# Attention's probabilities transposed by VectorE squares and transfers through DRAM instead of by TensorE

## The chip, the cores and the metric

The kernel runs on one core of one Trainium2 chip. The metric is device microseconds of one execution; less is better. The engines are named as in the profile: PE is TensorE's matmul (PEld its weight load), DVE is VectorE, ACT is ScalarE, POOL is GpSimd, SP is SyncE. POOL and SP issue the DMAs spoken of here, each from a queue of its own.

## The reference

One decoder block on 512 tokens of width 1024 in float32: an input projection feeds a dilated sliding-window attention and a Mamba-2 mixer, both are gated, summed and projected, and a squared-ReLU MLP follows. The change is in the attention, 12 heads of width 64:

```python
scores = einsum(q, k) * dh ** -0.5 - slope * distance      # causal, three (window, dilation) patterns
p = exp(scores - max)
att = sum over patterns of (p @ v, weighted by its denominator) / sum of the denominators
```

The three patterns see the same keys, so the kernel adds to the scores the distance term and the logarithm of how many patterns hold a pair of positions, and takes one softmax over at most 512 keys.

## The kernel before

Nearly every matrix product is made of float32 operands split into a high and a low half, three matmuls of 128x512 each (`three`, L235; `split`, L95). PE's order is the program's: `mm` and `tr` keep their instructions in program order. DVE, ACT and POOL instructions are placed by the scheduler of the language, by priorities and its own estimate of when things are ready, and each engine then runs its list in order. Weights come by DMA from SP's queue in pieces of 1 MB, double-buffered, and are split by ACT and DVE (`wh_`, `wl_`).

The attention stage lies at about 76 to 232 us of the span. Its work per head `h`:

- `head_scores(h)` (L576): POOL makes a `strip` (distance times slope, L579, plus mask, L580). PE makes the scores of four query tiles of 128 rows, causal, so tile `i` has `(i+1)*128` columns (`pq`, eight matmuls). DVE adds the strip and takes the row extremum (L596), ACT takes the exponential (L598), DVE the reciprocal (L600) and the scaling of four pieces (L603). The result `s` has 1280 columns: query on the partition, key along the row.
- `head_transpose(h)` (L605): PE transposes ten 128x128 squares of `s` into three PSUM banks `pt` (L230 is the helper's line), and ACT copies them to `pT` (L615): key on the partition.
- `pair_values(p)` (L617): for heads `2p` and `2p+1`, PE multiplies `pT` by the values `vtok`, eight matmuls into `po`.

Between these, `fill.run(us)` puts matmuls of input projections (`psq`, `psk`, `psga`, `psgs`, `psz`) into PE's order, up to about that many microseconds by a cost in the code (`FILLA`, `FILLB`, `FILLC`: 3.0, 2.8, 2.8). The loop over heads calls `head_scores(h + 1)`, fills, transposes head `h`, and in every even iteration from 2 on the values of the pair before; the last pair's values lie in `att_unit(0)`, behind its first 15 matmuls (`psap`).

Of the kernel before, what the change touches and what calls it, by code (L numbers as in the profile page):

```python
# [11 lines left out]
F32 = mybir.dt.float32  # L12
F32R = mybir.dt.float32r
AF = mybir.ActivationFunctionType
ALU = mybir.AluOpType
# [3 lines left out]
P = 128  # L19
T = 512  # L20
NT = 4
D = 1024
KD = D // P
NH = 12
# [59 lines left out]
def hybrid_block(ctx: ExitStack, tc: tile.TileContext, a: dict):  # L84
    nc = tc.nc
    act, dve, pool, pe, sp = nc.scalar, nc.vector, nc.gpsimd, nc.tensor, nc.sync
# [139 lines left out]
    def mm(*args, **kw):  # L226
        tc.keep_in_program_order(pe.matmul(*args, **kw))  # L227

    def tr(dst, src):
        tc.keep_in_program_order(pe.transpose(dst, src, ident))  # L230
# [17 lines left out]
    def hbuf(name, dt=F32, tag="hA"):  # L248
        return hp.tile([P, T], dt, name=name, tag=tag)
# [8 lines left out]
    def abank(name):  # L258
        return psa.tile([P, T], F32, name=name, tag="a")
# [8 lines left out]
    vtok = vp.tile([P, NT, AW], F32, name="vtok")  # L268
# [9 lines left out]
    with tc.tile_pool(name="start", bufs=1, reuse_waits="tile") as st:  # L278
# [117 lines left out]
        dist = load_const("dist", [P, T], a["dist"], vp)  # L396
        mask = load_const("mask", [P, T], a["mask"], vp)
# [44 lines left out]
        t = [vp.tile([P, GROUPS, NT, HG], F32, name=f"dt{j}") for j in range(4)]  # L442
# [62 lines left out]

    att = [(hbuf(f"ah{p}", F32R), hbuf(f"al{p}", F32R)) for p in range(NH // 2)]

    SOFF = {3: 0, 2: 512, 0: 896, 1: 1024}
    POFF = {0: 0, 1: 512, 3: 896, 2: 1024}
    BANKS = ((0, 512), (512, 1024), (1024, 1280))  # L510
    actx = ExitStack()
    ap = actx.enter_context(tc.tile_pool(name="attn", bufs=2, side="right", reuse_waits="tile"))

# [57 lines left out]

        return in_unit(f"{n}{d}", evac)

    probs, pT, outs = {}, {}, {}

    def head_scores(h):  # L576

        strip = ap.tile([P, T], F32, name=f"strip{h}", tag="strip", bufs=2)
        pool.tensor_scalar(strip, dist, SLOPES[h], None, ALU.mult)  # L579
        pool.tensor_tensor(strip, strip, mask, op=ALU.add)  # L580
        s = probs[h] = ap.tile([P, 1280], F32, name=f"s{h}", tag="s", bufs=2)
        st = ap.tile([P, 3, NT], F32, name=f"st{h}", tag="st", bufs=2)
        for grp in ((3,), (2, 0), (1,)):
            pq = abank(f"pq{h}_{grp[0]}")
            base = SOFF[grp[0]]
            for i in grp:
                n = (i + 1) * P
                o = SOFF[i] - base
                isl = slice(i * P, (i + 1) * P)
                mm(pq[:, o : o + n], qs[h][:, isl], kh[h][:, 0:n], start=True, stop=False)  # L590
                mm(pq[:, o : o + n], qs[h][:, isl], kl[h][:, 0:n], start=False, stop=True)
            for i in grp:
                n = (i + 1) * P
                o = SOFF[i] - base
                sv = s[:, SOFF[i] : SOFF[i] + n]
                dve.tensor_tensor_reduce(sv, pq[:, o : o + n], strip[:, T - n : T], 1.0, 3e38,  # L596
                                         ALU.add, ALU.min, st[:, 0, i : i + 1])
                act.activation(sv, sv, AF.Exp, bias=st[:, 0, i : i + 1], scale=-1.0,  # L598
                               accum_out=st[:, 1, i : i + 1])
        dve.reciprocal(st[:, 2, :], st[:, 1, :])  # L600
        for i in range(NT):
            sv = s[:, SOFF[i] : SOFF[i] + (i + 1) * P]
            dve.tensor_scalar(sv, sv, st[:, 2, i : i + 1], None, ALU.mult)  # L603

    def head_transpose(h):  # L605
        s = probs.pop(h)
        pT[h] = ap.tile([P, 1280], F32, name=f"pT{h}", tag="pT", bufs=3)
        for b, grp in enumerate(((0,), (1, 3), (2,))):
            b0, b1 = BANKS[b]
            pt = abank(f"pt{h}_{b}")  # L610
            for j in grp:
                for i in range(j, NT):
                    c = POFF[j] - b0 + (i - j) * P
                    tr(pt[:, c : c + P], s[:, SOFF[i] + j * P : SOFF[i] + (j + 1) * P])
            act.activation(pT[h][:, b0:b1], pt[:, : b1 - b0], AF.Copy)  # L615

    def pair_values(p):  # L617
        po = abank(f"po{p}")
        for j in (0, 1, 3, 2):
            n = T - j * P  # L620
            for half in range(2):
                h = 2 * p + half
                mm(po[64 * half : 64 * half + 64, j * P : T], vtok[:, j, h * 64 : (h + 1) * 64],
                   pT[h][:, POFF[j] : POFF[j] + n], start=j == 0, stop=j == 2)
        split(po, att[p][0], att[p][1])
# [353 lines left out]
    for j in range(2):  # L979
        w = take(f"o{j}")  # L980
# [284 lines left out]
    j = last  # L1265
# [49 lines left out]
    for j in range(nu - 2):  # L1315
        w = take(f"dn{j}")
# [55 lines left out]
```

## Time and profile before

| | |
|---|---|
| median of 3 runs | 1086.67 us (1086.59 to 1087.11) |
| the profiled execution, its own time | 1087.34 us |
| its span, first to last instruction | 1085.6 us |
| instructions | 14723 |
| POOL's instructions, busy | 87, 72.0 us |
| DMA moved | 113.06 MB, mean 104 GB/s |

Times in the profile are microseconds from the span's start unless marked ns. Rows of a timeline give start, duration, engine, line and operation, `out<-in`, the shape, and in brackets idle time before it with what ended it; rows of groups give busy time, mean ns of one, and idle time with its releaser. A matmul's duration overlaps the next one's, so steps from start to start tell what it costs. DMA issues do not count as busy time of POOL or SP; the time to landing is counted from the issue.

### The profile page before, as it was taken

To read this page: it belongs to the slowest core of one execution; us is meant where nothing else is said; L and a number is where in the kernel's file an instruction comes from. 1 tells how busy PE (TensorE), PEld (TensorE's weight loads), DVE (VectorE), ACT (ScalarE), POOL (GpSimd) and SP (SyncE) were. 2 spreads that over 40 slices of the span, in tenths; PEclk is the share of its full clock that TensorE was granted. 3 is DMA by queue.
4 is the path that set the end of the run, shared out by engine and by line. 5 is a ranking of instruction groups with operands and counts; after the bars stand their busy time and mean duration, and the time that the engine had idled before them with its cause. 6 is when DMAs were issued, how large, how long until landed. Compare 5 with 4: busy or idle time off the path is not lost.

```text
span 1085.6 us, 14723 instructions
## 1 busy us (share of the span) xinstructions
PE 1074.3 (99%) x5959; PEld 915.7 (84%) x5959; DVE 732.2 (67%) x1096; ACT 535.5 (49%) x921; POOL 72.0 (7%) x87
## 2 busy tenths in 40 slices
PE   9999999999999999999999999999999999999997
PEld 8988787778888888888888878889899998888886
DVE  6657666436777878797979795868677785242324
ACT  6356656526375645547373723454467665332222
POOL 2203122000000010100000000000000000000000
PEclk9999999999999999999999999999999999999999
DMA  8232122322433332333434223540233324333202
GB/s 276 86 100 78 59 78 68 100 76 90 134 88 117 88 126 78 126 83 122 126 103 130 88 80 124 189 160 1 78 117 117 117 80 141 110 120 114 82 35 78
DMA packets 87654, 113.06 MB, mean 104 GB/s; under 512 B 4625, under 2 KB 74769, under 8 KB 86561
## 3 DMA queue, kind: packets, MB, share of 16 engines
q1 hardware_dynamic: 85216, 101.01, 28.9%
q0 software_dynamic: 2224, 11.09, 3.1%
q8 instruction: 47, 0.77, 0.3%
q14 instruction: 23, 0.18, 0.1%
q10 hardware_dynamic: 144, 0.00, 0.0%
HBM read 109.92 MB, written 2.18 MB: 103 GB/s over the span
## 4 chain that ended last, share of the span: by engine, by line
PE 92%; DVE 4%; DMA 2%; ACT 1%; issue 1%; SPq 0%; POOL 0%; POOLq 0%; DVEq 0%; ACTq 0%
PE psd L227 16%; PE psx L227 8%; PE psz L227 8%; PE psbc L227 8%; PE pssp L227 7%; PE psuX L227 6%; PE psu L227 4%; PE psga L227 4%; PE psgs L227 4%; PE psk L227 3%; PE psq L227 3%; PE psuZ L227 3%; PE psv L227 3%; PE psap L227 3%; PE psuY L227 1%; PE pq L227 1%
## 5 line engine op out<-in xcount | busy, mean ns | idle before, releaser
L227 PE MATMUL psd<-wh_dn,hh 128*128 128x512 f32 x240 | 93.4, 389 | 0.0
L227 PE MATMUL psd<-wl_dn,hh 128*128 128x512 f32 x240 | 93.4, 389 | 0.0
L227 PE MATMUL psd<-wh_dn,hl 128*128 128x512 f32 x240 | 93.4, 389 | 0.0
L99 DVE TENSOR_TENSOR hl<-hidden,hh 128x512 fp32r<-128x512 f32 x31 | 21.1, 692 | 71.4 <-ACT hh L96 71.3
L96 ACT ACTIVATE hh<-hidden 128x512 fp32r<-128x512 f32 x31 | 19.1, 628 | 92.0 <-PE psd L227 92.0
L227 PEld LDWEIGHTS psd<-wh_dn,hl 128*128 128x128 f32 x240 | 45.0, 188 | 9.4
L227 PEld LDWEIGHTS psd<-wh_dn,hh 128*128 128x128 f32 x240 | 45.0, 188 | 9.4
L227 PEld LDWEIGHTS psd<-wl_dn,hh 128*128 128x128 f32 x240 | 45.0, 188 | 9.2
L842 ACT ACTIVATE sq<-y 128x512 f32<-128x512 f32 x16 | 17.8, 1120 | 70.5 <-DVE y L839 70.4
L227 PE MATMUL psz<-uh,wh_z 128*128 128x512 f32 x128 | 51.1, 399 | 0.0
L227 PE MATMUL pssp<-yth,wh_sp 128*128 128x512 f32 x128 | 50.9, 398 | 0.0
L227 PE MATMUL psx<-uh,wl_x 128*128 128x512 f32 x128 | 50.0, 390 | 0.7 <-DVE wl_x L99 0.7
L227 PE MATMUL psx<-uh,wh_x 128*128 128x512 f32 x128 | 50.6, 396 | 0.0
L227 PE MATMUL pssp<-yth,wl_sp 128*128 128x512 f32 x128 | 50.1, 392 | 0.0
L227 PE MATMUL psz<-uh,wl_z 128*128 128x512 f32 x128 | 50.0, 391 | 0.0
L227 PE MATMUL pssp<-ytl,wh_sp 128*128 128x512 f32 x128 | 49.9, 390 | 0.0
L227 PE MATMUL psbc<-uh,wh_bc 128*128 128x512 f32 x128 | 49.9, 390 | 0.0
L227 PE MATMUL psz<-ul,wh_z 128*128 128x512 f32 x128 | 49.9, 390 | 0.0
L227 PE MATMUL psx<-ul,wh_x 128*128 128x512 f32 x128 | 49.8, 389 | 0.0
L227 PE MATMUL psbc<-uh,wl_bc 128*128 128x512 f32 x128 | 49.8, 389 | 0.0
L227 PE MATMUL psbc<-ul,wh_bc 128*128 128x512 f32 x128 | 49.8, 389 | 0.0
L693 DVE SCALAR_TENSOR_TENSOR ch<-psx,cw,ch 128x511 f32<-128x511 f32 (+2 forms) x48 | 35.6, 742 | 20.4 <-ACT ch L691 19.7
(361 smaller groups left out, 3253.9 us busy)
## 6 DMA issues: line engine op xcount, KB each, us to landing
ws_up<-in_w_up_dram SPq DMA_DIRECT2D x16, 1024.0 KB, 5.5
ws_dn<-in_w_down_dram SPq DMA_DIRECT2D x15, 1024.0 KB, 5.0
ws_z<-in_w_in_dram SPq DMA_DIRECT2D x8, 1024.0 KB, 7.1
ws_x<-in_w_in_dram SPq DMA_DIRECT2D x8, 1024.0 KB, 5.2
w<-acs_d POOLq DMA_DIRECT2D x8, 1024.0 KB, 5.4
ws_bc<-in_w_in_dram SPq DMA_DIRECT2D x16, 512.0 KB, 4.7
ws_sp<-in_w_ssm_proj_dram SPq DMA_DIRECT2D x8, 1024.0 KB, 4.9
ws_ga<-in_w_in_dram SPq DMA_DIRECT2D x4, 1024.0 KB, 6.2
```

The lines of the kernel that those rows point to most:

```text
L96: ins = act.activation(hi, src, AF.Copy)
L99: ins = (eng or dve).tensor_tensor(lo, src, hi.bitcast(F32), op=ALU.subtract)
L227: tc.keep_in_program_order(pe.matmul(*args, **kw))
L693: dve.scalar_tensor_tensor(h[:, d:], ps[:, : T - d], cw[:, ct, 3 - d : 4 - d], h[:, d:], op0=ALU.mult, op1=ALU.add)
L842: pin(act.activation(q.rearrange("n (j b p) -> n j b p", j=NT, b=4), y.rearrange("n (j p b) -> n j b p", j=NT, b=4), AF.Square, scale=1.0 ...
```

## The change

Line numbers of the changed kernel differ from those of the one before: there L606, L610 and L613 are the DVE steps of the scores, L582 and L583 the strip, L630 the DVE transposes, L635 the writes, L641 the reads.

`head_transpose` now belongs to the end of `head_scores` and holds no PE or ACT work. DVE transposes 32x32 squares of `s` with five instructions into one buffer `sqt` (`bufs=1`, 1536 columns, zeroed once). Eight POOL DMAs write it to two DRAM tiles `p_d`, 32 partitions each; four POOL DMAs read these back into `pT`, so that whole 128x128 blocks end up transposed, with the queries in another order. `pair_values` writes `po` through a strided view, and the split behind it puts the order right. The strip of head `h + 1` is made by `make_strip` at the start of `head_scores(h)`; `s` has one buffer in place of two. The values of a pair come one iteration earlier.

```diff
-    SOFF = {3: 0, 2: 512, 0: 896, 1: 1024}
-    POFF = {0: 0, 1: 512, 3: 896, 2: 1024}
+    SOFF = {1: 0, 0: 256, 2: 384, 3: 768}
+    POFF = {0: 0, 1: 512, 2: 896, 3: 1152}
...
+    sqt = ap.tile([P, 1536], F32, name="sqt", tag="sqt", bufs=1)
+    pool.memset(sqt, 0.0)
...
+    def make_strip(h):
+        strip = strips[h] = ap.tile([P, T], F32, name=f"strip{h}", tag="strip", bufs=2)
         pool.tensor_scalar(strip, dist, SLOPES[h], None, ALU.mult)
         pool.tensor_tensor(strip, strip, mask, op=ALU.add)
...
+    def head_transpose(h, s):
+
+        for n0, tiles, kt in ((SOFF[0], 1, 0), (SOFF[1], 3, 0), (SOFF[1], 3, 1), (SOFF[2], 2, 2), (SOFF[3], 1, 3)):
...
+            dve.transpose(dst, src)
+        rows_ = [dram.tile([2 * P, 4 * w], F32, name=f"p_d{h}_{w}") for w in (P, 64)]
+        for b, w in enumerate((P, 64)):
+            for r in range(4):
+                rs_ = slice(32 * r, 32 * r + 32)
+                pool.dma_start(rows_[b][:, r * w : (r + 1) * w].rearrange("(m i) x -> i m x", i=32),
+                               sqt[rs_, 1024 * b : 1024 * b + 8 * w].rearrange("i (m x) -> i m x", x=w))
         pT[h] = ap.tile([P, 1280], F32, name=f"pT{h}", tag="pT", bufs=3)
-        for b, grp in enumerate(((0,), (1, 3), (2,))):
-            b0, b1 = BANKS[b]
-            pt = abank(f"pt{h}_{b}")
-            for j in grp:
-                for i in range(j, NT):
-                    c = POFF[j] - b0 + (i - j) * P
-                    tr(pt[:, c : c + P], s[:, SOFF[i] + j * P : SOFF[i] + (j + 1) * P])
-            act.activation(pT[h][:, b0:b1], pt[:, : b1 - b0], AF.Copy)
+        for kt in range(4):
+            n = 4 - kt
+            src = rows_[kt // 2][(kt % 2) * P : (kt % 2) * P + P, :].rearrange("p (r x) -> p r x", r=4)
+            pool.dma_start(pT[h][:, POFF[kt] : POFF[kt] + n * P].rearrange("p (r x) -> p r x", r=4),
+                           src[:, :, 32 * (kt % 2) :])
...
-        head_transpose(h)
-        if h % 2 == 0 and h > 0:
+        if h % 2 == 1 and h < NH - 1:
             fill.run(FILLB)
-            pair_values(h // 2 - 1)
+            pair_values(h // 2)
             fill.run(FILLC)
```

The order shows three places. PE, before, where the third head's squares are transposed (`s_1004`, into `pt`) between matmuls of a projection (`psk`):

```order
L227 MATMUL psk_1_1148<-ul,wh_k_960 128x512
L227 MATMUL psk_1_1148<-uh,wl_k_961 128x512
L230 MATMUL pt_0_1159<-ident,s_1004 128x128 x4
L230 MATMUL pt_1_1165<-ident,s_1004 128x128 x4
L230 MATMUL pt_2_1171<-ident,s_1004 128x128 x2
```

PE, now, around the first pair's values (`po`, from `pT` of heads 0 and 1):

```order
L227 MATMUL psk_0_1113<-ul,wh_k_988 128x512
L227 MATMUL psk_0_1113<-uh,wl_k_989 128x512
L227 MATMUL po_1120<-pT_894,vtok 64x512
L227 MATMUL po_1120<-pT_964,vtok 64x512
L227 MATMUL po_1120<-pT_894,vtok 64x4x96
L227 MATMUL po_1120<-pT_964,vtok 64x4x96
L227 MATMUL po_1120<-pT_894,vtok 64x4x32
L227 MATMUL po_1120<-pT_964,vtok 64x4x32
L227 MATMUL po_1120<-pT_894,vtok 64x4x64
```

The groups of `pt` are gone from PE. Between the last score matmul of head 1 and `po` of pair 0 there stand 69 matmuls of projections and the eight of head 2's scores; for the pairs behind it 72, 69, 69 and 66 projection matmuls, and for the last pair 54, with no scores among them. Between the last score matmul of pair `p`'s odd head and the first one of the next odd head there are 81 of them, two groups of scores and one `po`, or a few more.

POOL, before, in the same part of the program: the strips of heads 2 to 4 and nothing else.

```order
L643 DMA acs_d<-acsT 128x128
L579 TENSOR_SCALAR strip_1001<-dist 128x512
L580 TENSOR_TENSOR strip_1001<-strip_1001,mask 128x512
L579 TENSOR_SCALAR strip_1101<-dist 128x512
L580 TENSOR_TENSOR strip_1101<-strip_1101,mask 128x512
L579 TENSOR_SCALAR strip_1234<-dist 128x512
```

POOL, now, around head 3 (`p_d_128_1177`, `p_d_64_1178`, `pT_1187`); `strip_1143` is head 4's, `strip_1268` head 5's:

```order
L641 DMA pT_1073<-p_d_64_1064 128x4x32
L582 TENSOR_SCALAR strip_1143<-dist 128x512
L635 DMA p_d_128_1177<-sqt 32x8x128
L583 TENSOR_TENSOR strip_1143<-strip_1143,mask 128x512
L635 DMA p_d_128_1177<-sqt 32x8x128 x3
L635 DMA p_d_64_1178<-sqt 32x8x64 x4
L641 DMA pT_1187<-p_d_128_1177 128x512
L641 DMA pT_1187<-p_d_128_1177 128x4x96
L641 DMA pT_1187<-p_d_64_1178 128x256
L641 DMA pT_1187<-p_d_64_1178 128x4x32
L582 TENSOR_SCALAR strip_1268<-dist 128x512
```

Twelve DMAs of a head now stand between the strips in POOL's queue, and half of head 4's strip stands behind head 3's first write, which waits for DVE's transposes. The first read waits for the first four writes, the third for the last four.

DVE, before, in head 3 (`s_1104`): the scaling, the low halves of keys (`kl`), then `po`'s low half.

```order
L600 RECIPROCAL st_1105<-st_1105 128x4
L603 TENSOR_SCALAR s_1104<-s_1104,st_1105 128x128
L603 TENSOR_SCALAR s_1104<-s_1104,st_1105 128x256
L603 TENSOR_SCALAR s_1104<-s_1104,st_1105 128x384
L603 TENSOR_SCALAR s_1104<-s_1104,st_1105 128x512
L570 TENSOR_TENSOR kl_1143<-psk_0_1082,kh_1142 64x512 x2
L99 TENSOR_TENSOR al_650<-po_1187,ah_649 128x512
```

DVE, now, in head 3 (`s_1146`):

```order
L613 TENSOR_SCALAR s_1146<-s_1146,st_1147 128x384
L613 TENSOR_SCALAR s_1146<-s_1146,st_1147 128x512
L570 TENSOR_TENSOR kl_1205<-psk_0_1113,kh_1204 64x512 x2
L630 STREAM_TRANSPOSE sqt<-s_1146 128x4x32
L630 STREAM_TRANSPOSE sqt<-s_1146 128x3x4x32 x2
L99 TENSOR_TENSOR wl_q_1250<-ws_q_1247,wh_q_1249 128x1024
L570 TENSOR_TENSOR kl_1236<-psk_1_1210,kh_1235 64x512 x2
L99 TENSOR_TENSOR wl_q_1250<-ws_q_1247,wh_q_1249 128x1024
L630 STREAM_TRANSPOSE sqt<-s_1146 128x2x4x32
L570 TENSOR_TENSOR kl_1242<-psk_1_1210,kh_1241 64x512 x2
L630 STREAM_TRANSPOSE sqt<-s_1146 128x4x32
```

Five transposes came in, with splits of a weight and of keys between them. The first waits until the head before has landed its first four writes, the fourth for the other four, since `sqt` is one buffer; the splits behind a waiting transpose wait with it. In head 7 a weight's and two keys' splits stand between the scaling and the transposes; in heads 5, 9 and 11 there is little or nothing.

More of the change, by code (lines that the diff above doesn't have):

```diff
@@ L506, in hybrid_block @@
     att = [(hbuf(f"ah{p}", F32R), hbuf(f"al{p}", F32R)) for p in range(NH // 2)]
-    SOFF = {3: 0, 2: 512, 0: 896, 1: 1024}
-    POFF = {0: 0, 1: 512, 3: 896, 2: 1024}
-    BANKS = ((0, 512), (512, 1024), (1024, 1280))
+    SOFF = {1: 0, 0: 256, 2: 384, 3: 768}
+    POFF = {0: 0, 1: 512, 2: 896, 3: 1152}
     actx = ExitStack()
@@ L572, in qk_unit, with head_scores @@
         return in_unit(f"{n}{d}", evac)
-    probs, pT, outs = {}, {}, {}
-    def head_scores(h):
-        strip = ap.tile([P, T], F32, name=f"strip{h}", tag="strip", bufs=2)
+    pT = {}
+    sqt = ap.tile([P, 1536], F32, name="sqt", tag="sqt", bufs=1)
+    pool.memset(sqt, 0.0)
+    strips = {}
+    def make_strip(h):
+        strip = strips[h] = ap.tile([P, T], F32, name=f"strip{h}", tag="strip", bufs=2)
         pool.tensor_scalar(strip, dist, SLOPES[h], None, ALU.mult)
         pool.tensor_tensor(strip, strip, mask, op=ALU.add)
-        s = probs[h] = ap.tile([P, 1280], F32, name=f"s{h}", tag="s", bufs=2)
+    make_strip(0)
+    def head_scores(h):
+        strip = strips.pop(h)
+        if h + 1 < NH:
+            make_strip(h + 1)
+        s = ap.tile([P, 1280], F32, name=f"s{h}", tag="s", bufs=1)
         st = ap.tile([P, 3, NT], F32, name=f"st{h}", tag="st", bufs=2)
@@ L584, in head_scores @@
             pq = abank(f"pq{h}_{grp[0]}")
-            base = SOFF[grp[0]]
             for i in grp:
                 n = (i + 1) * P
-                o = SOFF[i] - base
+                o = 3 * P if i == 0 else 0
                 isl = slice(i * P, (i + 1) * P)
@@ L593, in head_scores @@
                 n = (i + 1) * P
-                o = SOFF[i] - base
+                o = 3 * P if i == 0 else 0
                 sv = s[:, SOFF[i] : SOFF[i] + n]
@@ L603, in head_scores @@
             dve.tensor_scalar(sv, sv, st[:, 2, i : i + 1], None, ALU.mult)
-    def head_transpose(h):
-        s = probs.pop(h)
-        pT[h] = ap.tile([P, 1280], F32, name=f"pT{h}", tag="pT", bufs=3)
-        for b, grp in enumerate(((0,), (1, 3), (2,))):
-            b0, b1 = BANKS[b]
-            pt = abank(f"pt{h}_{b}")
-            for j in grp:
-                for i in range(j, NT):
-                    c = POFF[j] - b0 + (i - j) * P
-                    tr(pt[:, c : c + P], s[:, SOFF[i] + j * P : SOFF[i] + (j + 1) * P])
-            act.activation(pT[h][:, b0:b1], pt[:, : b1 - b0], AF.Copy)
+        head_transpose(h, s)
@@ new lines, in head_transpose @@
+    def head_transpose(h, s):
+        for n0, tiles, kt in ((SOFF[0], 1, 0), (SOFF[1], 3, 0), (SOFF[1], 3, 1), (SOFF[2], 2, 2), (SOFF[3], 1, 3)):
+            first = 0 if n0 == SOFF[0] else 4 - tiles
+            src = s[:, n0 + kt * P : n0 + kt * P + (tiles - 1) * 3 * P + P]
+            if tiles > 1:
+                src = bass.AP(tensor=src.tensor, offset=src.offset,
+                              ap=[src.ap[0], [3 * P, tiles], [32, 4], [1, 32]])
+            else:
+                src = src.rearrange("p (q c j) -> p q c j", q=1, j=32)
+            w = P if kt < 2 else 64
+            dst = sqt[:, 1024 * (kt // 2) + 4 * w * (kt % 2) : 1024 * (kt // 2) + 4 * w * (kt % 2) + 4 * w]
+            q0 = first if kt < 2 else first - 2
+            dst = dst.rearrange("p (c q j) -> p q c j", c=4, j=32)[:, q0 : q0 + tiles]
+            dve.transpose(dst, src)
[5 more added lines that the diff above has]
+                               sqt[rs_, 1024 * b : 1024 * b + 8 * w].rearrange("i (m x) -> i m x", x=w))
+        pT[h] = ap.tile([P, 1280], F32, name=f"pT{h}", tag="pT", bufs=3)
+        for kt in range(4):
[3 more added lines that the diff above has]
+                           src[:, :, 32 * (kt % 2) :])
@@ L617, in pair_values @@
     def pair_values(p):
         po = abank(f"po{p}")
+        pov = po.rearrange("p (r x) -> p r x", r=4)
         for j in (0, 1, 3, 2):
@@ L622, in pair_values @@
                 h = 2 * p + half
-                mm(po[64 * half : 64 * half + 64, j * P : T], vtok[:, j, h * 64 : (h + 1) * 64],
-                   pT[h][:, POFF[j] : POFF[j] + n], start=j == 0, stop=j == 2)
-        split(po, att[p][0], att[p][1])
+                mm(pov[64 * half : 64 * half + 64, :, 32 * j :], vtok[:, j, h * 64 : (h + 1) * 64],
+                   pT[h][:, POFF[j] : POFF[j] + n].rearrange("p (r x) -> p r x", r=4), start=j == 0, stop=j == 2)
+        split(po.rearrange("p (r q j) -> p q r j", r=4, q=4), *(t.rearrange("p (q r j) -> p q r j", r=4, q=4)
+                                                                for t in att[p]))
     sz0 = []
```

## The prediction

> **What bounds the kernel now.** I read the busy times and slices first, then the waits, then the timeline of the stage that changes. The page's lines:
>
> ```profile
> span 1085.6 us, 14723 instructions
> PE 1074.3 (99%) x5959; PEld 915.7 (84%) x5959; DVE 732.2 (67%) x1096; ACT 535.5 (49%) x921; POOL 72.0 (7%) x87
> PEclk9999999999999999999999999999999999999999
> ```
>
> TensorE is busy for 99% of the span at full granted clock. The attention stage, from the windows view (PE, PEld, DVE, ACT, POOL busy, clock, DMA share, GB/s), and the longest waits of PE in the whole run:
>
> ```profile
> 12.00:14.00 2.00, 1.25 (x10) 0.84 (x8) 2.00 (x5) 0.92 (x3) 0.00 (x0) 1.00 1.03 404
> 80.00:232.00 152.00, 152.00 (x785) 121.20 (x784) 90.66 (x207) 87.18 (x192) 28.75 (x21) 1.00 0.26 80
> PE warm L227 <- POOL ones L218: 1.2, 1, 1.2
> PE ut L230 <- DVE un L334: 1.1, 1, 1.1
> ```
>
> In those 152 us PE never waits: each PE instruction taken out there shortens the run, and each microsecond that PE is made to wait lengthens it. DVE has 61 us free, POOL over 120 us, DMA three quarters. The first row shows DMA moving 404 GB/s, five times the stage's 80.
>
> **What is removed.** Ten transposes of each head on PE (start, duration):
>
> ```profile
> 121.31 0.39 PE L227 MATMUL psga<-ul,wh_ga 128*128 128x512 f32 x1
> ...
> 124.28 0.39 PE L227 MATMUL psga<-uh,wl_ga 128*128 128x512 f32 x1
> 124.51 1.25 PE L230 MATMUL pt<-ident,s 128*128 128x128 f32 x10
> 125.52 0.48 PE L227 MATMUL psga<-uh,wh_ga 128*128 128x512 f32 x1
> 125.83 0.40 PE L227 MATMUL psga<-ul,wh_ga 128*128 128x512 f32 x1
> ```
>
> The rows from 121.31 to 124.28 are 13 steps of 0.2285 us, the price of a full matmul. From 124.51 to 125.83 are 1.32 us with one full matmul in it, so a group costs 1.09 us, and 12 heads give **-13.1 us**, all on the path. The 36 copies of ACT go too:
>
> ```profile
> L615 ACT ACTIVATE pT<-pt 128x512 f32<-128x512 f32 (+1 forms) x36 | 16.4, 524 | 5.9 <-PE pt L230 5.8
> ```
>
> Their 16.4 us lay beside PE, which did not wait: worth nothing. The values matmuls keep their column counts (512, 384, 256, 128, now in four strided pieces): 0.
>
> **What is added on DVE.** Five transposes a head. The nearest rows: one DVE transpose of 128 columns, and a DVE operation by width:
>
> ```profile
> L854 DVE STREAM_TRANSPOSE pnt<-pn x8: 304/306/317, 304.3 to 655.3; 128x128 f32<-128x128 f32 x8
> L596 DVE CUSTOM_DVE_ANT_0 s<-pq,strip 128x512 f32<-128x512 f32 x11 | 7.6, 688 | 8.3 <-PE pq L227 8.3
> L596 DVE CUSTOM_DVE_ANT_0 s<-pq,strip 128x128 f32<-128x128 f32 x11 | 3.1, 285 | 0.0
> ```
>
> 688 less 285 over three widths is 134 ns per 128 columns, so 306, 574, 574, 440 and 306 ns: 1.45 us for the first three, 2.2 us for all, 26 us in the stage. DVE goes from 91 to 117 of 152 us; PE covers it. Without that cover it is part of the chain below.
>
> **What is added on POOL, and the wait it makes.** Twelve DMAs a head: eight writes of 256 contiguous runs each (512 B or 256 B), then reads of 128, 512, 128 and 512 runs. The trace has only DMAs of 128 runs; POOL's rows, and the time to landing:
>
> ```profile
> 68.58 0.76 POOL L643 DMA_DIRECT2D acs_d<-acsT  x1 [23.38 <-DVE acsT L642]
> 125.24 1.49 POOL L579 TENSOR_SCALAR strip<-dist 128x512 f32<-128x512 f32 x1 [14.34 <-DVE st L596]
> 126.81 1.35 POOL L580 TENSOR_TENSOR strip<-strip,mask 128x512 f32<-128x512 f32 x1
> 306.76 0.61 POOL L859 DMA_DIRECT2D rt_d<-rt  x1 [0.30 <-POOL rt L215]
> 309.41 0.56 POOL L861 DMA_DIRECT2D rg<-rt_d  x1 [2.04 <-DMA rt_d<-rt]
> rg<-rt_d POOLq DMA_DIRECT2D x8, 256.0 KB, 3.6
> rt_d<-rt POOLq DMA_DIRECT2D x8, 2.0 KB, 1.9
> acs_d<-acsT POOLq DMA_DIRECT2D x1, 64.0 KB, 2.8
> ```
>
> A read that depends on a write starts 2.65 us after it (306.76 to 309.41). An issue of 128 runs costs 0.55 to 0.76 us. What 256 and 512 cost is unknown: 0.55 if runs are free; 1.5 and 2.2 if the cost grows with them in full (2 x 0.76, 4 x 0.55). I take 0.76 for a write (acs_d has the same 512 B runs), 0.55 for the plain reads and 0.9 for the cut ones, and keep both ends. How long the scores take to become scaled probabilities, PE's last score matmul and DVE's scaling, in a head with other DVE work between and in one without:
>
> ```profile
> 120.95 0.28 PE L227 MATMUL pq<-kl,qs 128*128 128x256 f32 x1
> 126.46 2.32 DVE L603 TENSOR_SCALAR s<-s,st 128x128 f32<-128x128 f32 x4
> 172.52 0.28 PE L227 MATMUL pq<-kl,qs 128*128 128x256 f32 x1
> 175.48 2.30 DVE L603 TENSOR_SCALAR s<-s,st 128x128 f32<-128x128 f32 x4
> ```
>
> That is 7.5 us (121.23 to 128.78) and 5.0 us. The chain of an odd head, clean: 5.0 scaled, 1.45 three transposes, 1.33 the strip's addition behind the first write on POOL, 8 x 0.76 = 6.1 writes: 13.9 us. The third read waits for the last write, 2.65 after that issue began (13.1): 15.75. Its issue 0.55, the fourth lands 3.6 after its start: **19.9 us**, or 22.4 with other DVE work.
>
> PE's own work from the end of the odd head's scores to `po`: by the order 72, 69, 69 and 66 full matmuls and one group of scores (1.35 us) for pairs 1 to 4, so 17.8, 17.1, 17.1 and 16.4 us. The order puts other DVE work into heads 3 and 7, little into 5 and 9. Waits: 22.4 - 17.8 = 4.6, 19.9 - 17.1 = 2.8, 5.3, 3.5: 16.2 us. Pair 0: heads 0 and 1 score only 5.4 us apart, and POOL serves head 0 first: its writes begin at 84.7 (scores end at 78.1), end at 90.8, third read 92.7, last issue ends 94.1; head 1's writes end at 100.2, its third read starts at 102.1, data at 106.2. PE is there at 83.5 + 17.1 = 100.6: 5.6 us. Last pair: 54 full matmuls, 12.3 us, against 19.9 - 1.33 (no strip left) = 18.6: 6.3 us. Sum of waits **+28.1 us**.
>
> POOL's own sum per head is 6.1 + 1.1 + 1.8 + 2.8 = 11.8 us plus about 1.3 us of waiting for landings, within PE's period of 11.8 us (half of 81 full matmuls, two score groups and 2.4 us of `po`) plus the waits. The single `sqt` makes DVE's next transposes wait until the writes have landed, some 10 us after they were ready; heads are 11 us apart or more, so this holds at these prices, and DVE's queue behind it (the low halves of the weights) is not delayed. Bytes: 1.4 MB a head, 117 GB/s beside 80: under the 404 seen.
>
> **Sum.** -13.1 + 28.1 = +15.0 us. The profiled execution took 1087.34 us (span 1085.6 and 1.7 around it), 0.67 above the median of the runs, so 1102.3 for its like and 1086.67 + 15.0 = **1102 us** as a median.
>
> The Trainium skill, *DMA: Bandwidth & Descriptors*, section on one DMA by the gpsimd path, gives about 2.0 us plus bytes over 436 GB/s per DMA. By it a write lands in 2.3 us and the last read in 2.15, each chain is 1.8 us shorter, and the sum would be about +4 us. The trace's 2.65 and 3.6 us are longer, and its numbers are kept above.
>
> **Rivals.**
> - *Hidden after all (faster).* Issues at 0.55, landings at 1.9 and 2.8, scaling in 4.5: 4.5 + 1.45 + 1.33 + 4.4 = 11.7; third read 13.05; data at 16.4, not later than PE anywhere but at the last pair (15.1 against 12.3: 2.8 us). Net -10 us, 1076. For it: the rows at 0.55 and 1.9. Against: they move less or in longer runs. It decides when the six waits together stay under 13.1 us.
> - *POOL becomes the bound.* Writes at 1.1, cut reads at 1.5: 8.8 + 1.1 + 3.0 = 12.9 us a head and 2.8 for nine strips: 180 us from 84.7, data of head 11 at 267. Without waits `po` of the last pair would start at 214.5 (227.6 before, less 13.1). Net 267 - 227.6 = +39, 1126; with the full doubling some +95. It decides when a head costs POOL more than 13 us, that is a write above 0.85. For it: twice to four times the runs of any row.
> - *PE restarts slowly.* The first matmuls of the kernel, and the same ones later:
>
> ```profile
> 1.16 5.73 PE L227 MATMUL warm<-ones 128*128 128x128 f32 x28 [1.16 <-POOL ones L218]
> 8.64 0.83 PE L227 MATMUL warm<-ones 128*128 128x128 f32 x6
> ```
>
> 28 in 5.57 us (to the next start at 6.73) is 199 ns each, against 0.58 / 6 = 97 ns (8.64 to 9.22): about half pace after standing still. If each of the six waits brings back some 3.5 us at half pace, 1.7 us is lost each time: +10, 1112. For it: waits of 3 to 6 us where before none passed 1.2. The Trainium skill, *TensorE: Matmul & The Clock Gate*, Part 1, states this: half clock after an idle window of about 3.4 us, full after as long a busy one. The 199 ns agree with the cold half.
>
> **Chances.** Forecast, +3 to +30: 0.52. PE restarts slowly: 0.08. POOL-bound: 0.17. Hidden: 0.15. Gain and waits cancel: 0.08. A difference of 0.2% (2.2 us) is about what can be told from no change. So faster 0.15, same 0.08, slower 0.77. The range leaves out a tenth at either end, most of the hidden case below and of the doubled prices above: 1080 to 1148.
>
> **What would show it.** No `pt` on PE; PE idle before six `po`, by DMA `pT`, 3 to 6 us each; POOL's writes near 0.76, cut reads near 0.9; DVE transposes of 0.3 to 0.6 us; the rest of the span as before. Writes at 1 us or more, or DVE waiting for `p_d` ahead of its transposes, would prove me too low; `po` without a wait, too high.

## The result, and the profile after

The changed kernel takes 1104.1 us (median of four, 1101.8 to 1106.6) where the kernel before took 1086.8 beside it: a ratio of 1.0159 with a 95% interval of 1.0137 to 1.0181, 17.3 us slower. The profiled execution took 1103.85 us, its span 1102.0. The lines of the page that answer to those of before (span, busy times, granted clock by slices):

```profile
span 1102.0 us, 14769 instructions
PE 1073.3 (97%) x5839; PEld 907.2 (82%) x5839; DVE 748.0 (68%) x1156; ACT 519.4 (47%) x885; POOL 161.0 (15%) x232
PEclk9999999989999999999999999999999999999999
```

PE has 120 instructions fewer and is busy almost as long as before (1073.3 against 1074.3 us): what it saved is given back as slower work, and the span has 16.4 us more on top. POOL's busy time, other than the section on the profile before says, does count its DMA issues: in the attention stage 56.2 us are writes, 31.5 reads and 28.1 strips. The windows view puts it in the attention stage (PE, PEld, DVE, ACT, POOL busy, clock, DMA share, GB/s), and the view of waits, for that stage, says for what:

```profile
80.00:250.00 170.00, 152.33 (x670) 113.70 (x669) 105.76 (x266) 71.17 (x156) 115.68 (x165) 0.96 0.63 172
PE po L227 <- DMA pT<-p_d: 17.7, 10, 3.2
POOL p_d L635 <- DVE sqt L630: 27.4, 10, 6.2
POOL pT L641 <- DMA p_d<-sqt: 7.0, 8, 2.0
```

Where PE was busy for every microsecond, it is now idle for 17.7 of 170 (170.00 less 152.33), all of it at `po`, for `pT`. The DMA engines' share went from 0.26 at 80 GB/s to 0.63 at 172. POOL, the engine that issues, was busy for 115.68 of the 170 us; most of the rest it stood waiting for DVE, 27.4 us of it for the transposes. From the start of each values group to its end, less the 2.4 us that it takes without a wait, PE lost 5.7, 3.3, 4.1, 6.1, 1.4 and 6.6 us at the six pairs, 27.2 in all; 28.1 had been forecast (5.6, 4.6, 2.8, 5.3, 3.5, 6.3). For 17.7 of these 27.2 us PE stood still; in the other 9.5 it is recorded as busy longer than such groups are elsewhere.

The last pair's chain from end to end, in the order of time (PE's last score matmul, DVE's scaling and transposes, POOL's writes and reads, PE's values):

```profile
223.46 0.28 PE L227 MATMUL pq<-kl,qs 128*128 128x256 f32 x1
226.68 1.27 DVE L613 TENSOR_SCALAR s<-s,st 128x128 f32<-128x128 f32 x4
227.87 0.76 DVE L630 STREAM_TRANSPOSE sqt<-s 128x128 f32<-128x128 f32 x2
228.56 0.65 DVE L543 SCALAR_TENSOR_TENSOR sz<-sz,psz 128x512 f32<-128x512 f32 x1
229.13 1.08 DVE L630 STREAM_TRANSPOSE sqt<-s 128x384 f32<-128x384 f32 x3
229.98 4.63 POOL L635 DMA_DIRECT2D p_d<-sqt  x8 [3.00 <-DVE sqt L630]
235.28 2.70 POOL L641 DMA_DIRECT2D pT<-p_d  x4 [0.67 <-issue]
235.95 1.07 PE L227 MATMUL po<-pT,vtok 128*64 128x512 f32 x2
238.51 1.07 PE L227 MATMUL po<-pT,vtok 128*64 128x512 f32 x4 [1.50 <-DMA pT<-p_d]
241.07 1.14 PE L227 MATMUL po<-pT,vtok 128*64 128x384 f32 x4 [1.48 <-DMA pT<-p_d]
243.42 1.54 PE L227 MATMUL po<-pT,vtok 128*64 128x128 f32 x6 [1.22 <-DMA pT<-p_d]
```

PE's last scores end at 223.74 and the last data lands at 243.38: 19.6 us, where the forecast's chain for this pair was 18.6. Prices of the parts: minimum, median and maximum in ns of one transpose, one write and one read, and median landing times.

```profile
L630 DVE STREAM_TRANSPOSE sqt<-s x60: 262/404/578, 84.7 to 229.9; 128x128 f32<-128x128 f32 x24, 128x384 f32<-128x384 f32 x24, 128x256 f32<-128x256 f32 x12
L635 POOL DMA_DIRECT2D p_d<-sqt x96: 582/584/732, 86.2 to 234.0; - x96
L641 POOL DMA_DIRECT2D pT<-p_d x48: 549/682/767, 91.7 to 237.2; - x48
p_d<-sqt POOLq DMA_DIRECT2D x48, 128.0 KB, 2.8
pT<-p_d POOLq DMA_DIRECT2D x12, 192.0 KB, 3.8
pT<-p_d POOLq DMA_DIRECT2D x12, 64.0 KB, 5.1
```

Issuing was cheaper than taken (a write 0.58, not 0.76; a cut read 0.75, not 0.9), and the last landing dearer: 5.1 us at the median for the fourth read of a head, though it is the smallest. That median hides two cases. The same read behind the same three others lands in 2.3 to 3.0 us in heads 1, 2, 3, 6 and 9, and in 5.5 to 6.1 us in heads 0, 4, 5, 7, 10 and 11. In the six late ones 0.8 to 1.05 MB of weights for the projections, issued by SP, moved while the reads were under way, in the five early ones 0.2 MB or none; head 8 (4.7 us) fits neither. Here are the last two reads in an early head, 3 (DMA view from 131.9 to 135 us), and in a late one, 7, with the weights beside them (185.7 to 192.2):

```profile
pT<-p_d POOLq DMA_DIRECT2D x1, 128.0 KB, 2.2
pT<-p_d POOLq DMA_DIRECT2D x1, 64.0 KB, 2.3
```

```profile
ws_ap<-in_w_att_proj_dram SPq DMA_DIRECT2D x1, 768.0 KB, 6.9
pT<-p_d POOLq DMA_DIRECT2D x1, 128.0 KB, 5.0
pT<-p_d POOLq DMA_DIRECT2D x1, 64.0 KB, 5.8
```

So the last part of a chain meets the weights or misses them. This goes by what the rows show together; no run moved a weight's transfer away. In the last head's stretch the windows view has a DMA share of 0.95 at 270 GB/s:

```profile
235.00:245.00 10.00, 5.81 (x22) 1.93 (x20) 0.78 (x1) 0.00 (x1) 3.14 (x5) 0.83 0.95 270
```

The granted clock fell to 0.50 three times in the stage. The 3.4 us ahead of the first and of the last fall, and the three stretches at the low clock:

```profile
101.60:105.00 3.40, 0.73 (x4) 0.20 (x4) 3.34 (x8) 1.22 (x4) 3.02 (x5) 1.00 0.58 182
238.10:241.50 3.40, 1.50 (x8) 0.40 (x8) 0.00 (x0) 0.00 (x0) 0.42 (x1) 1.00 1.16 300
105.00:108.40 3.40, 3.40 (x13) 1.64 (x12) 2.27 (x11) 1.66 (x7) 0.68 (x1) 0.50 0.95 289
193.70:197.10 3.40, 3.40 (x9) 2.67 (x9) 0.69 (x1) 0.00 (x0) 1.18 (x2) 0.50 0.05 13
241.50:248.30 6.80, 5.58 (x17) 3.46 (x15) 0.69 (x1) 0.60 (x1) 0.00 (x0) 0.50 0.60 203
```

What the second of them costs, after pair 3:

```profile
193.53 0.46 PE L227 MATMUL psga<-uh,wl_ga 128*128 128x512 f32 x1
193.79 0.63 PE L227 MATMUL psga<-uh,wh_ga 128*128 128x512 f32 x1
...
197.18 0.39 PE L227 MATMUL psga<-uh,wl_ga 128*128 128x512 f32 x1
```

From 193.79 to 197.18 eight full matmuls take 0.424 us each instead of 0.2285: 1.6 us lost after the wait has ended. About as much is lost behind the last pair, whose group ends at 244.96; the stretch from 105.0 lies almost whole inside pair 0's group (100.04 to 108.13) and is counted there.

### The profile page after: what moved, and what is told of

Read it like the earlier page. It is cut to its first block, busy times and chain, and to the rows that moved or that the text cites. A ratio compares the mean times of both kernels' runs of the same rounds, so it can differ in the third digit from the quotient of the medians.

```text
span 1102.0 us, 14769 instructions
## 1 busy us (share of the span) xinstructions
PE 1073.3 (97%) x5839; PEld 907.2 (82%) x5839; DVE 748.0 (68%) x1156; ACT 519.4 (47%) x885; POOL 161.0 (15%) x232
## 4 chain that ended last, share of the span: by engine, by line
PE 81%; DMA 6%; DVE 6%; POOL 2%; issue 2%; ACT 2%; POOLq 0%; SPq 0%; DVEq 0%; ACTq 0%
PE psd L227 15%; PE psx L227 8%; PE psbc L227 8%; PE psz L227 8%; PE pssp L227 7%; PE psuX L227 6%; PE psu L227 4%; PE psgs L227 3%; PE psuZ L227 3%; PE psv L227 3%; PE psap L227 3%; DMA pT<-p_d 2%; PE psk L227 2%; DMA p_d<-sqt 2%; PE psga L227 2%
## 5 line engine op out<-in xcount | busy, mean ns | idle before, releaser
L635 POOL DMA_DIRECT2D p_d<-sqt x96 | 56.2, 593 | 27.6 <-DVE sqt L630 27.4
```

The lines of the kernel that those rows point to most:

```text
L635: pool.dma_start(rows_[b][:, r * w : (r + 1) * w].rearrange("(m i) x -> i m x", i=32), sqt[rs_, 1024 * b : 1024 * b + 8 * w].rearrange("i ...
```

## The experiments

Twelve kernels were run, each beside the kernel before on the same chip (1086.9 to 1087.2 us there), so the ratios are compared.

**1 (none). What the removal alone is worth.** The values multiply a constant `pTc`, and nothing is transposed:

```diff
-        head_transpose(h, s)
-                   pT[h][:, POFF[j] : POFF[j] + n]...
+                   pTc[:, POFF[j] : POFF[j] + n]...
```

> The changed kernel without its second half: the probabilities are not transposed at all (no DVE transposes, no writes, no reads), and the values matmuls multiply a constant tile of zeros of the same shape, so nothing waits. The output is therefore not attention's. It prices the removal alone. Theory: 12 groups of ten PE transposes at 1.09 us are gone and nothing comes in their place, so 1086.7 - 13.1 = 1073.6 us (1072.5 to 1075). Rival: PE was held by something else in part of those groups (a weight load, an eviction), so that less comes back: over 1077 us.

Measured: 1073.24 us, ratio 0.9874 (0.9861 to 0.9888), within the theory's range. The page's span, with PE busy for 99% of it again:

```profile
span 1071.5 us, 14445 instructions
PE 1060.4 (99%) x5839; PEld 903.2 (84%) x5839; DVE 732.2 (68%) x1096; ACT 519.8 (49%) x885; POOL 74.6 (7%) x89
```

13.7 us are gained against 13.1 forecast. So the ten PE transposes of a head were all on the path, and what the change puts in their place costs 1104.1 - 1073.2 = 30.9 us.

**2 (nowait). The new work, with nobody waiting for it.** The same constant in the values, but all transposes, writes and reads stay; `pT` has two buffers:

> The changed kernel with all its DVE transposes, writes and reads, but the values matmuls multiply a constant tile of zeros instead of what is read back, so PE never waits for the chain (pT has two buffers instead of three, to make room for the constant; the output is not attention's). Theory: the work on DVE, POOL and the DMA engines hides beside PE, so the time is that of the kernel without it, 1073.6 us (1072.5 to 1076), and all that the changed kernel loses is the wait for the data and what follows from it: 27 us of waiting and some 4 of slow clock. Rival: the side load itself costs PE time, by low halves of the weights that DVE delivers late, by weight or score evictions behind the transposes, or by DMA contention with the weights: 1077 to 1090 us, with waits of PE at places other than po.

Measured: 1095.42 us, ratio 1.0081 (1.0067 to 1.0095). The rival was right in kind, and by more than its range (1077 to 1090): 22.2 us over the run without transposes although PE waits for no read at all. The view of waits of PE in the stage, and the clock by slices:

```profile
PE pq L227 <- DVE st L608: 13.8, 7, 4.1
PEclk9999898999999999999999999999999999999999
```

PE now waits at the scores' banks, which DVE empties late, seven times up to 4.1 us, and in the stage (80 to 232 us) its granted clock is 0.93 on the mean, so part of the loss is slow clock. So the forecast's picture, a chain that is late for PE while DVE and POOL have time to spare, lacks something: the side work alone holds PE up. In the changed kernel the waits view has no such wait; PE, held at `po`, probably came to the scores late enough.

**3 (warm). Does the wait cost clock?** Matmuls of no use fill the waits:

```diff
+        for _ in range({0: 18, 1: 12, 2: 15, 3: 22, 4: 4, 5: 24}[p]):
+            mm(po, uh[:, 0, 0:P], uh[:, 0, :], start=True, stop=True)
```

> The changed kernel with matmuls of no use (18, 12, 15, 22, 4 and 24 of 0.2285 us, into the bank that the values overwrite) in front of the six values groups, where PE waits; each fills most of a wait, so PE is not idle for 3 us anywhere in the stage. Theory that the waits also cost clock: the 0.59 of full clock that the windows show for about 4 us after three of the waits goes, about 1.6 us at each, so 1104.1 - 5 = 1099 us (1097.5 to 1101). Rival, that only the idle time counts and the lower clock in the records has no cost of its own: 1104 us (1102.5 to 1106), or a little more where a dummy group outlasts its wait.

Measured: 1108.5 us, ratio 1.0195 (1.018 to 1.021). Neither: 4.4 us slower. The waits for `pT` fell only from 17.7 to 8.2 us for 21.7 us of added matmuls, because the data came later too: in the first pair the reads of the second head began at 102.5 instead of 101.2 us, and the fourth of them landed at 110.2 instead of 106.4, in 5.8 us instead of 3.0, with 1.05 MB of weights moving beside it instead of 0.2. Every later head starts from there. As a test of the clock it decides nothing; run 12 asks again where nothing follows that depends on PE.

**4 (late). More time for each chain.** The values one iteration of the head loop later, a fourth `pT` buffer, the strips in buffers that only the last pair's output needs:

```diff
-        if h % 2 == 1 and h < NH - 1:
+        if h % 2 == 0 and h > 0:
             fill.run(FILLB)
-            pair_values(h // 2)
+            pair_values(h // 2 - 1)
```

> The changed kernel with the values of a pair one iteration of the head loop later, where the kernel before had them (after the scores of head 2p+3 instead of 2p+2), so that a head's chain has a further PE period of about 11.8 us to end in. That needs a fourth pT buffer; room for it is made by keeping the two strips in two of the heap's buffers that the last pair's output takes only at its end. The last pair is not moved. Theory (the chain's lag, about 19 to 22 us a head, is the cause, and its throughput is enough): the waits of the first five pairs, 20.6 us in the profile, go with their slow clock of about 3 us, the last one of 6.6 us stays: 1104.1 - 23.6 = 1080.5 us (1078.5 to 1083). Rival (POOL's throughput is the cause: some 11.5 us a head with its waits for landings against a PE period that is now 11.8): the waits come back one pair later and at the last pair, which waits for over 12 us: 1086 us or more.

Measured: 1106.73 us, ratio 1.0186 (1.017 to 1.0202): no faster than the change itself. The lag alone, on which my whole sum rested, is refuted as the single cause. The waits of PE, and of DVE for the strips:

```profile
PE po L227 <- DMA pT<-p_d: 14.1, 4, 9.7
PE pq L227 <- DVE st L607: 5.9, 4, 2.1
DVE s L607 <- POOL strip L584: 9.8, 6, 4.6
```

The first five pairs did what the theory said: beyond 2.4 us each, their groups lost 4.8 us together instead of 20.6. The waits came back elsewhere, as the rival said: 12.0 us at the last pair (9.7 and 2.3), 5.9 at the scores, and there DVE had been waiting 9.8 us for strips that stood in POOL's queue behind reads. The rival's reason, that POOL is full, does not follow: in the same stage POOL itself waited 20.2 us for transposes and 14.7 us for writes to land. Head 11's strip, for which DVE waited 4.6 us, began at 220.80; POOL had stood still for 3.6 us just before, at a read whose writes had not landed. It is the order of the queue that these rows show.

**5 and 6 (strip, late_s). POOL's queue relieved.** One edit on the changed kernel (5, with one strip buffer in place of two), and on the kernel of run 4 (6):

```diff
-        pool.tensor_scalar(strip, dist, SLOPES[h], None, ALU.mult)
-        pool.tensor_tensor(strip, strip, mask, op=ALU.add)
+        dve.scalar_tensor_tensor(strip, dist, SLOPES[h], mask, op0=ALU.mult, op1=ALU.add)
```

> The changed kernel with one edit: each head's strip is made by DVE in one instruction (about 0.7 us, one buffer) instead of two by POOL (1.49 + 1.3 us). Theory (POOL's queue is what the heads stand in line for, at some 11.5 us a head): 2.8 us less of POOL per head, and no strip between the first write and the second, shortens every chain by 1.3 us at least, and the six waits at po together by 8 to 14 us: 1104.1 - 11 = 1093 us (1090 to 1097). Rival (POOL is not the limit; DVE, which delivers its transposes late, is, and gets 0.7 us a head more to do): 1102 us or more.

> The kernel of run late (values one head later) with the strips made by DVE instead of POOL. In run late PE waited 5.9 us at the scores' bank, because DVE waited 9.8 us for strips that stood behind reads in POOL's queue, and 9.7 us at the last pair, because POOL was behind by then. Theory (POOL's throughput): without the strips a head costs POOL about 8.7 us with its waits against PE's 11.8, so POOL keeps up: the waits at the scores go, pairs 0 to 4 don't wait, the last waits 5 to 7 us: 1073.2 + 7 and 1 to 3 of slow clock = 1082 us (1079 to 1086). Rival (DVE's late transposes set the chain, whoever makes the strips): 1095 us or more.

Measured: 1097.48 us (ratio 1.0096, 1.0082 to 1.011) and 1089.47 us (1.0021, 1.0012 to 1.003). On the changed kernel the edit is worth 6.6 us, less than the 8 to 14 expected; with the later values it is worth 17, but 1089.47 is above the theory's range (1079 to 1086) and below the rival's 1095. Later values alone gave nothing, the strips alone 6.6, both 14.6: two limits in a row, and lifting the first shows the second. Whether it is the strips' place in the queue or their 2.8 us a head that counts, these two runs do not separate. With both, one long wait is left, at the last pair, and the values after it are slow (14 matmuls in 4.53 us):

```profile
PE po L227 <- DMA pT<-p_d: 11.0, 3, 10.1
227.78 4.53 PE L227 MATMUL po<-pT,vtok 128*64 128x512 f32 x14 [10.11 <-DMA pT<-p_d]
```

**7 (late3). Run 6 with 30 matmuls ahead of the last pair's values instead of 15.**

> As run late_s, and the last pair's values behind 30 matmuls of the first part of the next projection instead of 15, so 3.4 us later on PE. Theory: the last wait shrinks by those 3.4 us and what slow clock follows from it: 3 to 5 us less than late_s, 1078 us (1075 to 1082), faster than the kernel before. Rival: the last wait is not set by the lag but by what DVE and POOL still have in line; then the time is that of late_s within 1 us.

Measured: 1087.42 us, ratio 1.0003 (0.9994 to 1.0012). The last wait fell by 3.9 us to 6.2 in the profile, the median time by 2.1, less than the 3 to 5 expected and more than the rival's 1; the runs of the two kernels overlap (1085.7 to 1089.3 here, 1088.1 to 1090.6 before). Neither forecast was met.

**8 and 9 (nowait_s, nowait_2). What is left of the side load.** Run 2 with the strips on DVE (8), then with two buffers for `s` besides (9; the change had made it one) and, to make room, one for `pT`:

> The kernel of run nowait (all the transposes and transfers are made, but the values multiply a constant tile of zeros, so nobody waits for what is read back; the output is not attention's) with the strips made by DVE instead of POOL. In run nowait PE lost 22 us to the side load, 14 of it in waits at the scores' bank behind DVE. Theory (DVE waits for POOL's queue: for strips, and for sqt to be written out): without the strips the queue is short enough, and the time comes to within 1 to 6 us of the run with no transposes: 1074 to 1080 us. Rival (DVE is blocked by its own order, the transposes and the output's low half standing ahead of the scores): 1088 us or more.

> The kernel of run nowait_s (nobody waits for what is read back; strips by DVE; the output is not attention's), with two buffers for the scores s, as the kernel before the change had, instead of one; pT has one buffer for that. In nowait_s 12.6 us were left over the run without transposes, 8.5 of it waits of PE at the scores' bank for DVE. Theory (with one s DVE can't read the next head's scores out of their banks until all five transposes of this head are through, and these stand behind split work in DVE's queue): with two, the waits at the scores go and the time is within 4 us of the run without transposes, 1074 to 1077 us. Rival (DVE is simply late, or the one sqt blocks it until its writes have landed): 1082 us or more.

Measured: 1085.80 us (ratio 0.9986, 0.9978 to 0.9995) and 1088.99 us (1.0024, 1.0014 to 1.0033). The first lies between theory and rival, the second is in the rival's range. The strips were 9.6 of the 22.2 us; 12.6 remain, 8.5 of them waits at the scores. With two `s` these waits fell to 2.7 us, as the theory said, but the time rose: nobody waits for the transposes in this kernel, so its last ones run at the start of the next stage, whose first work on DVE (`ch`) and whose transfer on POOL (`w`) stand behind them in the order, and PE waits there instead. The rows of DVE and POOL, and the waits of PE from 76 to 290 us in run 9:

```profile
246.04 1.55 DVE L631 STREAM_TRANSPOSE sqt<-s 128x384 f32<-128x384 f32 x4
247.51 3.98 DVE L723 SCALAR_TENSOR_TENSOR ch<-psx,cw,ch 128x511 f32<-128x511 f32 x6
255.60 0.55 POOL L784 DMA_DIRECT2D w<-acs_d  x1
PE ptx L230 <- DVE ct L727: 3.0, 1, 3.0
PE pq L227 <- DVE st L607: 2.7, 2, 1.4
PE psap L227 <- DVE ch L723: 2.4, 1, 2.4
```

So the single `s` is part of how DVE's lateness reaches the scores, and DVE's queue is a second line in which the heads stand; what the single `s` costs the changed kernel by itself stays open, because a kernel with later values has no room for a second `s`.

**10 and 11 (late4, late5). The last wait covered.** Run 7 with 45 matmuls ahead of the last pair's values (10), and less filling work after each head besides, `FILLA` 2.7 for 3.0, so that some of it is left for the end (11):

> As run late3 (values one head later, strips by DVE), with the last pair's values behind 45 matmuls of the next projection instead of 30: five of its six parts of three columns of the output are begun first, in three banks, then the values, then the sixth parts and the fourth column. In late3 PE waited 6.2 us for the last pair, its values group took 4.3 instead of 2.4 us, and the next part waited 0.9 us for the output's halves. Theory: all that is left of the loss is that one wait for the last head's chain, so 15 matmuls of 0.2285 us take 3.4 us from it, and some slow clock: 1083 us (1081.5 to 1084.5), faster than the kernel before by 0.3%. Rival: the last head's chain moves with PE (DVE or POOL are still behind by then), and the time stays at 1086 us or more.

> As run late4, with less of the other projections' work put after each head's scores (FILLA 2.7 instead of 3.0), so that more of it is left for the stretch between the last head's scores and its values: 102 matmuls (23.3 us) by the order, against 69 in late3, where the wait was 6.2 us. Theory: the last wait is covered whole and no other comes, since POOL and DVE need less than a period for a head once the strips are off POOL: 1073.2 and 2 to 4 for the first matmuls at low clock and small waits, 1077 us (1075 to 1080). Rival: with a shorter period (11 us) the heads' throughput on DVE and POOL is the bound again, and waits at the scores and at the earlier pairs give the time back: 1083 us or more.

Measured: 1084.55 us (ratio 0.9979, 0.997 to 0.9987) and 1088.23 us (1.0012, 1.0002 to 1.0021). Run 10, just above its theory's range, beats the kernel before by 0.2%, its last wait down to 3.8 us. Run 11 fell to its rival: the last wait is 1.3 us, but 2.4 came at the second pair, 1.9 at the scores and 1.0 at the fourth pair. With a shorter period the waits come back, so DVE, POOL and the transfers together seem to need about the period that they have; which of them, this run does not tell.

**12 (late4w). Clock, asked where nothing depends on PE afterwards.** Run 10 with 16 matmuls of no use where PE stood still:

```diff
+        for _ in range(16 if p == NH // 2 - 1 else 0):
+            mm(po, uh[:, 0, 0:P], uh[:, 0, :], start=True, stop=True)
```

> As run late4, with 16 matmuls of no use (3.66 us at 0.2285) into the last pair's bank in front of its values, where PE stood still for 3.83 us in late4; nothing before that place depends on PE any more, so the wait itself ends when it did. In late4 the values after the wait took 4.53 us for 14 matmuls at a granted clock of 0.50, against 2.37 us for all 16 elsewhere. Theory (standing still for 3 to 4 us costs clock afterwards, beside the wait): with PE busy through the wait the clock stays up, the values take 2.4 us and what follows runs at full pace: 2.4 us less, 1082.1 us (1081 to 1083.3). Rival (the slow values come from something else than the pause, their data's landing or the strided reading of pT): the time of late4, 1084.5 us (1083.5 to 1085.5).

Measured: 1081.53 us, ratio 0.9949 (0.9936 to 0.9963), about 3 us less than run 10, as the theory said (1081 to 1083.3), and the fastest of the kernels that do all the work. The values after the wait in run 10, its window from 229.2 to 233, and the same places of run 12:

```profile
229.26 4.53 PE L227 MATMUL po<-pT,vtok 128*64 128x512 f32 x14 [3.83 <-DMA pT<-p_d]
229.20:233.00 3.80, 3.74 (x13) 2.14 (x14) 0.00 (x0) 0.00 (x0) 0.14 (x1) 0.50 0.92 314
```

```profile
223.30 3.79 PE L227 MATMUL po<-uh 128*128 128x512 f32 x16
227.02 3.02 PE L227 MATMUL po<-pT,vtok 128*64 128x512 f32 x16
229.20:233.00 3.80, 2.89 (x15) 1.84 (x15) 1.44 (x3) 0.85 (x2) 0.00 (x0) 1.00 0.56 226
```

With PE kept busy the clock is 1.00 where it was 0.50, and the values take 3.02 us for 16 (0.65 more than elsewhere) instead of 4.53 for 14. In run 10 the last data landed at 230.86 us and the group ended 2.9 us later; in run 12 it landed at 229.13 and the group ended 0.9 us later. So standing still for 3.8 us costs about 2 us more afterwards by these rows. The times of the two runs differ by 3, but in the two profiled executions the last data also came 1.7 us earlier, so not all of the 3 is clock.

## Why the prediction came out, and which of its steps did not hold

- **The removal**: -13.1 forecast, -13.7 measured (run 1). The group price of 1.09 us from two start times was right, and so was costing ACT's copies at nothing.
- **The waits**: +28.1 forecast, 27.2 measured at the six `po`, each within 2.1 us of its forecast. That the two agree so closely is in part luck. What the forecast worked out is how long after PE's arrival the last data of a pair lands. By that measure (from the start of a pair's `po` to the landing of its odd head's fourth read) the six are 6.3, 4.8, 5.6, 7.6, 2.9 and 7.4 us, 34.6 in all. But PE multiplies the parts that are there while it waits for the rest, which the forecast left out, and so 7.4 us come back. PE's idle time at a pair was 0.7 to 4.9 us, where 3 to 6 had been named as the sign. The pieces of the working:
  - *Issue.* A write was taken at 0.76 us and costs 0.58; 256 runs cost no more than the 0.56 to 0.76 of 128. For eight writes that is 1.4 us a head too much. The bound "if runs are free" was nearer.
  - *Landing.* The last read was taken at 3.6 us. But for head 8 it lands in 2.3 to 3.0 us with few weights or none beside it and in 5.5 to 6.1 with them. The forecast compared bytes a second (117 beside 80, under 404) and saw room; it did not ask when the weights move. The odd heads 3 and 9 were early, and their pairs lost less than forecast (3.3 for 4.6, 1.4 for 3.5); heads 5, 7 and 11 were late, and theirs lost more (4.1 for 2.8, 6.1 for 5.3, 6.6 for 6.3). In the last head scaling, transposes and issues took 1.5 us less than forecast and the landing 2.5 us more.
  - *DVE.* The transposes are cheap (five in 1.74 us, 2.2 forecast). That the one `sqt` does not hold up DVE's queue came true: the waits view of the changed kernel has no wait of DVE for `p_d`. But other work of DVE stands between the parts of a head: from the end of the scaling to the fourth transpose it is 6.4 us in head 3 and 5.6 in head 9, 1.1 to 3.3 in the others. POOL's 27.4 us of waiting for transposes are no measure of this: in run 5 they are 58.7 us, and the kernel is faster.
  - *POOL.* "11.8 us a head, within PE's period" was too dear: by the measured prices a head costs POOL about 10.1 us (4.7 of writes, 2.6 of reads, 2.8 of strip), and the heads are 14 us apart (head 1's scores end at 83.1, head 11's at 223.7). What the sum over a head can't show is the order: a strip behind a read that waits for a landing makes DVE wait (run 4).
  - *Not in the sum.* The change makes `s` a single buffer. I did not cost that at all; runs 8 and 9 show it in the waits at the scores.
- **The rest**: 30.9 less 27.2 leaves 3.7 us, most of it slow clock behind pairs 3 and 5 (counted from 0). This is the mechanism of the rival "PE restarts slowly", at 1.6 us a time where 1.7 was priced, but after three waits, not six, and after one of the three inside the `po` group that was counted as wait. The Trainium skill's page *TensorE: Matmul & The Clock Gate*, Part 1, has half clock after about 3.4 us of idling. The traces agree in the clock (0.50) and in the length of the stretches at it (3.4, 3.4 and 6.8 us); but PE was not idle all through the 3.4 us ahead of them (busy 0.73 and 1.50 us in the rows above), and at the last pair no single wait was longer than 1.5 us. Here less than a whole idle window was enough.
- **The skill's other rule**, *DMA: Bandwidth & Descriptors*, about 2.0 us plus bytes over 436 GB/s for one DMA by gpsimd, would have put the last read at 2.15 us. It is a figure for one DMA: heads 1, 2, 3, 6 and 9 come near it (2.3 to 3.0 us), the late ones do not (5.5 to 6.1), and the measurement decides.
- **Rivals**: the hidden case needed the six waits under 13.1 us together; they were 27.2, or 17.7 by PE's idle time alone. POOL as the bound did not come, by its own condition (a write above 0.85 us) or by POOL's busy time (115.68 of 170 us).

The total was nearly right because errors of both signs met in the same six places: issues too dear, landings too cheap where weights moved, parts multiplied during the wait, and clock lost inside the groups. The mechanism, data that comes later than PE needs it, holds for the changed kernel. It is only the outermost of three limits, though: behind it lie the strips in POOL's queue (runs 4 to 6), and then, as far as runs 8 and 9 show, DVE's order with its single `s`. How much the weights' transfers cost by meeting the reads stays open.

## What to carry to other kernels

A stage in which one engine never waits gives back every instruction taken from it, but work moved from it to another engine and to memory needs two answers: when the last byte of a chain lands, and what stands in each queue on the way, and in which order: an engine with time to spare can still hold others up, when a short job stands in its line behind one that waits. Ask also which other transfers are under way when the chain's last one lands. When more lag does not help, look at what else stands in the queues: a small piece of work on the issuing engine, moved off (1.0186 to 1.0021 here), can be worth more than the lag. Then cover the last chain of a loop apart, since no later round hides it, and allow, after a wait of 3 or 4 us on TensorE, for 1.6 to 2 us of slow clock, which is what it cost in these traces.

## What the runs showed that I had not expected

- DMAs of 256 runs cost POOL 0.58 us to issue, no more than those of 128 (0.56 to 0.76 before the change); reads of 512 short runs took 0.75.
- The same 64 KB read lands in 2.3 to 3.0 us in five heads and in 5.5 to 6.1 in the six where 0.8 MB of weights or more move beside it.
- The clock was halved after two waits of 1.5 us, with 1.1 us of work between them (last pair), but not after a single one of 2.8 us (pair 2).
- A wait filled with useless matmuls is faster than the same wait left empty: 1.0 in clock against 0.50, and about 3 us of 1084. That was where nothing later depended on PE; in run 3, where later heads did, such matmuls cost 4.4 us.
